# Mixture of softmaxes: the first exponential of the first two units writes the output tile, and two early loads wait for less

## The chip, the cores and the metric

One core of one Trainium2 chip. The metric is the device time of one execution in microseconds. All runs here are of the fast state, at a granted clock of 1.0. The kernel before takes 780.76 us (median of 3, 780.73 to 780.80).

## The reference

```python
batch, seq, vocab, num_heads = 32, 128, 4096, 4
# logits (32, 128, 4, 4096) fp32, prior (32, 128, 4) fp32
prior_probs = softmax(prior)                       # over the 4 heads
softmax     = softmax(logits)                      # over the 4096 entries
mixture     = sum(prior_probs[..., None] * softmax, axis=2)   # (32, 128, 4096)
```

268.4 MB of logits come in and 67.1 MB go out. The reference subtracts the row maximum before the exponential; the kernel does without that on the logits.

## The kernel before

The 4096 rows (batch times sequence) are cut into U = 32 units of 128 rows, one row per partition. A unit is 128 x 4 x 4096 values, 8.39 MB. The input tile `ltile` has two slots, used in turn, so the load of unit u+2 overwrites the slot of unit u. Units 0 to 29 go this way:

```python
lt  = ltile[:, u % 2]
acc = obuf[:, u % 2]                       # output tile, two slots
es  = (lt[:, 0], ebuf1, ebuf2, ebuf3)      # where the four exponentials go
# ScalarE: es[h] = exp(lt[:, h]), row sum into dsum[:, u, h]
# VectorE: rden = 1 / dsum;  GpSimd: coeff = rden * prior probability
# VectorE: acc  = es[0] * coeff[0]                      the "scaling"  -> adds[u, 0]
#          acc += es[h] * coeff[h], h = 1, 2, 3         the "adds"     -> adds[u, h]
# SP issues the store of acc once adds[u, 3] is done
```

The first exponential is written back into the input slot itself. So the slot may only be overwritten once the scaling has read it, and that is what the next load into it waits for:

```python
ld = nc.scalar.dma_start(out=ltile[:, u % 2, h:to], in_=lg[u // J, u % J, :, h:to, :])
if u >= 2:
    only(ld, adds[u - 2, 0] if h == 0 else exps[u - 2, to - 1])   # waits for these alone
else:
    only(ld)
...
late = u + 2 < U - 3           # if late, the load is created in the next unit's loop and then
if u + 2 < U and not late:     # moved ahead of that unit's first exponential in ScalarE's stream
    load(u + 2)
```

Loads are issued from ScalarE's stream, stores (nearly all) from SP's.

The softmax here doesn't subtract the row's maximum and nothing guards it: scores larger than these inputs give would overflow.

Of the kernel before, what the change touches and what calls it, by code (L numbers as in the profile page):

```python
# [47 lines left out]
def kernel(  # L48
# [10 lines left out]
    B, S, H, V = logits.shape  # L59
# [6 lines left out]
    U = G * J  # L66
# [13 lines left out]
    def only(ins, *keep):  # L80
        for k in keep:
            tc.add_manual_dep(
                ins.ins,
                k.ins.name,
                mybir.DependencyInfo(mybir.DependencyClass.Sync, mybir.DependencyReason.DATA),
                reason="all that this instruction waits for",
            )
        tc.declare_no_dep(
            ins.ins,
            group="loop",  # L90
            keep=[k.ins for k in keep] + before.get(ins.ins.engine, []),
            reason="covered by the waits that are kept",
        )
        tc.add_to_no_dep_group("loop", ins.ins)
        before[ins.ins.engine] = [ins.ins]
        return ins
# [4 lines left out]
    exps = {}  # L101
# [3 lines left out]
    def load(u):  # L105
        if u == 0 or u >= U - 3:
            cuts = (0, 2, 3, 4) if u == U - 1 else (0, 2, 4)
        else:
            cuts = (0, H)
        for h, to in zip(cuts, cuts[1:]):  # L110
            ld = nc.scalar.dma_start(  # L111
                out=ltile[:, u % 2, h:to], in_=lg[u // J, u % J, :, h:to, :]
            )


            if u >= 2:
                only(ld, adds[u - 2, 0] if h == 0 else exps[u - 2, to - 1])
            else:
                only(ld)
            for k in range(h, to):  # L120
                loads[u, k] = ld

    def store(u, acc, eng, lo=0, hi=V):
        st = eng.dma_start(out=ov[u // J, u % J, :, lo:hi], in_=acc[:, lo:hi])
        stores[u] = only(st, adds[u, H - 1])
# [10 lines left out]
    dsum = cpool.tile([P, U, H], FP32, name="dsum")  # L136
    rden = cpool.tile([P, U, H], FP32, name="rden")
    coeff = cpool.tile([P, U, H], FP32, name="coeff")



    ebuf1 = cpool.tile([P, V], FP32, name="ebuf1")
    ebuf2 = psum.tile([P, V], FP32, name="ebuf2")
    ebuf3 = cpool.tile([P, V], FP32, name="ebuf3")
    obuf = cpool.tile([P, 2, V], FP32, name="obuf")

    with tc.manual_schedule():
        load(0)
        nc.sync.dma_start(out=pr, in_=pv)
        load(1)  # L150
        nc.vector.reduce_max(pmax, pr, axis=AX.X)  # L151
        nc.vector.tensor_sub(pr, pr, pmax.unsqueeze(2).to_broadcast([2 * G, P, H]))  # L152
        nc.scalar.activation(pr, pr, AF.Exp)  # L153
        nc.vector.reduce_sum(pmax, pr, axis=AX.X)  # L154
        nc.vector.reciprocal(pmax, pmax)  # L155
        nc.vector.tensor_mul(  # L156
            pn.rearrange("k h r -> k r h"), pr, pmax.unsqueeze(2).to_broadcast([2 * G, P, H])
        )
        pq = pn.rearrange("k h (p j) -> k j h p", j=J)
        for t in range(P // 32):  # L160
            c = 1 - t // 2
            nc.vector.transpose(  # L162
                pp[32 * t : 32 * (t + 1), :, :, c : c + 2 * G],
                pq[:, :, :, 32 * (t % 2) : 32 * (t % 2 + 1)],
            )

        late = False
        for u in range(U):
            bufd = u < U - 2
            lt = ltile[:, u % 2]  # L170
            acc = obuf[:, u % 2] if bufd else lt[:, 0]
            es = (lt[:, 0], ebuf1, ebuf2, ebuf3) if bufd else [lt[:, h] for h in range(H)]
            ppu = pp[:, u % J, :, 2 * (u // J) + 1]

            def exp(h, *keep):
                ex = nc.scalar.activation(  # L176
                    es[h], lt[:, h], AF.Exp, accum_out=dsum[:, u, h : h + 1]
                )
                keep = (loads[u, h],) + keep
                if bufd and u and h in (1, 2):  # L180
                    keep += (adds[u - 1, 1 if h == 1 else H - 1],)
                exps[u, h] = only(ex, *keep)

            def weigh(h, n, *keep):
                rc = nc.vector.reciprocal(rden[:, u, h : h + n], dsum[:, u, h : h + n])  # L185
                only(rc, exps[u, h + n - 1])
                mul = nc.gpsimd.tensor_mul(  # L187
                    coeff[:, u, h : h + n], rden[:, u, h : h + n], ppu[:, h : h + n]
                )
                return only(mul, rc, *keep)  # L190

            def add(h, mul, lo=0, hi=V):
                if h == 0:
                    st = nc.vector.tensor_scalar(  # L194
                        out=acc[:, lo:hi], in0=es[h][:, lo:hi], scalar1=coeff[:, u, h : h + 1],
                        scalar2=None, op0=ALU.mult,
                    )
                    adds[u, h] = only(st, mul)
                else:
                    st = nc.vector.scalar_tensor_tensor(  # L200
                        out=acc[:, lo:hi], in0=es[h][:, lo:hi], scalar=coeff[:, u, h : h + 1],
                        in1=acc[:, lo:hi], op0=ALU.mult, op1=ALU.add,
                    )
                    adds[u, h] = only(st, mul, adds[u, h - 1])



            free = (stores[u - 2],) if bufd and u >= 2 else ()

            if u < U - 4:  # L210
                sets = ((0, H),)
            elif u == U - 2:
                sets = ((0, 2), (2, 3), (3, 4))
            else:
                sets = ((0, 2), (2, 4))
            for h in range(H):
                if h == 2 and 0 < u < U - 3:
                    store(u - 1, obuf[:, (u - 1) % 2], nc.sync)
                if h == 2 and u == U - 1:
                    store(u - 1, ltile[:, (u - 1) % 2, 0], nc.scalar)  # L220
                if h == 1 and late:
                    load(u + 1)
                    pairs.append((loads[u + 1, 0].ins, exps[u, 0].ins))
                    late = False
                exp(h, *(free if sets[0][1] == H and h == H - 1 else ()))
                g = next((g for g, to in sets if to == h + 1), None)
                if g is None:
                    continue
                mul = weigh(g, h + 1 - g, *(free if g == 0 and h < H - 1 else ()))
                for k in range(g, h + 1):  # L230
                    n = 2 if u == U - 1 and k == H - 1 else 1
                    w = V // n
                    for c in range(n):
                        add(k, mul, c * w, (c + 1) * w)
                        if n > 1:
                            store(u, acc, nc.scalar, c * w, (c + 1) * w)


            late = u + 2 < U - 3
            if u + 2 < U and not late:  # L240
                load(u + 2)

            if u == U - 2:
                for k in (u - 2, u - 1):
                    store(k, obuf[:, k % 2], nc.scalar)
# [30 lines left out]
```

## Time and profile before

| | before |
|---|---|
| time | 780.76 us |
| VectorE, ScalarE busy | 66%, 61% |
| DMA packets' share of 16 engines | 99.8% |
| rate over the span | 431 GB/s |
| load of unit 2: issued, load ahead of it landed | 32.18, 41.31 us |
| load of unit 3: issued, load ahead of it landed | 58.73, 64.51 us |

The first thing to ask of such a table is whether any engine is full. The compute engines are not; the DMA engines are. "Landed" is read in this text from where ScalarE starts on the data; a packet is a piece of a transfer, moved by one of the 16 engines.

### The profile page before, as it was taken

The page shows a single profiled execution, that of the slowest core. Times are in us where ns is not written, and L with a number is a line of the kernel's source. Part 1 is how long each engine was busy: PE and PEld are TensorE (multiplying, and loading weights), DVE is VectorE, ACT ScalarE, POOL GpSimd, SP SyncE. Part 2 cuts the span into 40 slices and gives each one's busy share as a digit, 9 for nine tenths or more (in the row PEclk, how much of TensorE's full clock was granted, in tenths as well). Part 3 has the DMA queues.
Part 4 walks back from the last instruction along what each step waited for, and adds up shares of the span by engine and source line. Part 5 has one row for each costly group of instructions (what it writes and reads, how often), then busy time and mean ns, then how long its engine had stood idle before and what let it go on. Part 6 is the DMA issues. An engine that isn't in the chain of part 4 may idle for free.

```text
span 779.1 us, 620 instructions
## 1 busy us (share of the span) xinstructions
DVE 517.7 (66%) x175; ACT 472.2 (61%) x258; POOL 7.6 (1%) x41
## 2 busy tenths in 40 slices
DVE  2447865568655686556875558755577555788986
ACT  4376555765557755577555675556755567557782
POOL 0000000000000000000000000000000000000000
DMA  9999999999999999999999999999999999999998
GB/s 407 458 417 400 475 404 431 431 465 424 404 468 401 463 417 423 452 448 414 417 468 407 458 404 468 421 413 448 416 459 417 457 405 464 410 429 431 432 428 379
DMA packets 10131, 335.64 MB, mean 431 GB/s; under 512 B 1136, under 2 KB 1136, under 8 KB 1168
## 3 DMA queue, kind: packets, MB, share of 16 engines
q10 hardware_dynamic: 6048, 276.83, 82.2%
q1 hardware_dynamic: 4080, 58.79, 17.6%
q14 instruction: 3, 0.02, 0.0%
HBM read 268.50 MB, written 67.11 MB: 431 GB/s over the span
## 4 chain that ended last, share of the span: by engine, by line
DMA 60%; DVE 28%; ACT 9%; issue 2%; POOL 0%; DVEq 0%; ACTq 0%; POOLq 0%
DMA out_dram<-obuf 47%; DVE obuf L200 23%; DMA ltile<-in_logits_dram 13%; ACT ebuf L176 8%; DVE obuf L194 4%; DVE ltile L200 1%; ACT ltile L176 1%; POOL coeff L187 0%; DVE rden L185 0%; DVEq L271 0%; ACTq L111 0%; POOLq L271 0%; ACTq L176 0%
## 5 line engine op out<-in xcount | busy, mean ns | idle before, releaser
L200 DVE SCALAR_TENSOR_TENSOR obuf<-ebuf,coeff,obuf 128x4096 f32<-128x4096 f32 x90 | 403.6, 4484 | 3.8 <-POOL coeff L187 0.6
L176 ACT ACTIVATE ebuf<-ltile 128x4096 f32<-128x4096 f32 x90 | 324.1, 3601 | 33.3 <-DVE obuf L200 19.4
L176 ACT ACTIVATE ltile<-ltile 128x4096 f32<-128x4096 f32 x38 | 137.4, 3615 | 255.4 <-DMA ltile<-in_logits_dram 255.0
L185 DVE RECIPROCAL rden<-dsum 128x4 f32<-128x4 f32 (+2 forms) x37 | 6.4, 174 | 235.9 <-ACT ebuf L176 233.2
L194 DVE TENSOR_SCALAR obuf<-ltile,coeff 128x4096 f32<-128x4096 f32 x30 | 70.6, 2353 | 10.9 <-POOL coeff L187 10.9
L200 DVE SCALAR_TENSOR_TENSOR ltile<-ltile,coeff 128x4096 f32<-128x4096 f32 (+1 forms) x7 | 27.0, 3874 | 1.0 <-POOL coeff L187 0.9
L176 ACT ACTIVATION_READ_ACCUMULATOR ebuf<-ltile 128x1 f32 x90 | 16.8, 187 | 0.0
L187 POOL TENSOR_TENSOR coeff<-rden,pp 128x4 f32<-128x4 f32 (+2 forms) x37 | 7.4, 201 | 756.2 <-DVE rden L185 745.6
L176 ACT ACTIVATION_READ_ACCUMULATOR ltile<-ltile 128x1 f32 x38 | 7.1, 186 | 0.0
L194 DVE TENSOR_SCALAR ltile<-ltile,coeff 128x4096 f32<-128x4096 f32 x2 | 4.7, 2353 | 0.6 <-POOL coeff L187 0.6
L153 ACT ACT_TABLE_LOAD x1 | 1.3, 1283 | 2.2 <-issue 2.2
L151 DVE TENSOR_REDUCE pmax<-pr 32x128 f32<-32x512 f32 x1 | 0.7, 674 | 2.5 <-DMA pr<-in_prior_dram 2.5
L162 DVE STREAM_TRANSPOSE pp<-pn 32x256 f32<-32x256 f32 x4 | 1.7, 435 | 0.1
L154 DVE TENSOR_REDUCE pmax<-pr 32x128 f32<-32x512 f32 x1 | 0.7, 674 | 0.7 <-ACT pr L153 0.7
L156 DVE TENSOR_TENSOR pn<-pr,pmax 32x512 f32<-32x512 f32 x1 | 1.0, 1019 | 0.0
L155 DVE RECIPROCAL pmax<-pmax 32x128 f32<-32x128 f32 x1 | 0.9, 941 | 0.0
L153 ACT ACTIVATE pr<-pr 32x512 f32<-32x512 f32 x1 | 0.6, 628 | 0.5 <-DVE pr L152 0.5
L152 DVE TENSOR_TENSOR pr<-pr,pmax 32x512 f32<-32x512 f32 x1 | 0.7, 679 | 0.0
L260 POOL MEMSET const-bfloat16-1.0<- 128x1 bf16 x1 | 0.1, 102 | 0.0
L260 POOL MEMSET const-uint8-127<- 128x1 uint8 x1 | 0.1, 102 | 0.0
L260 POOL MEMSET const-float32-0.0<- 128x1 f32 x1 | 0.1, 99 | 0.2 <-issue 0.2
L260 POOL MEMSET const-float32-1.0<- 128x1 f32 x1 | 0.1, 99 | 0.0
## 6 DMA issues: line engine op xcount, KB each, us to landing
out_dram<-obuf SPq DMA_DIRECT2D x28, 2048.0 KB, 28.1
ltile<-in_logits_dram ACTq DMA_DIRECT2D x7, 4096.0 KB, 25.5
ltile<-in_logits_dram ACTq DMA_DIRECT2D x2, 2048.0 KB, 30.9
out_dram<-obuf ACTq DMA_DIRECT2D x2, 2048.0 KB, 26.6
out_dram<-ltile ACTq DMA_DIRECT2D x1, 2048.0 KB, 19.3
out_dram<-ltile ACTq DMA_DIRECT2D x2, 1024.0 KB, 4.8
ltile<-in_logits_dram ACTq DMA_DIRECT2D x28, 29.6
pr<-in_prior_dram SPq DMA_DIRECT2D x1, 64.0 KB, 2.5
```

The source lines that it names most:

```text
L151: nc.vector.reduce_max(pmax, pr, axis=AX.X)
L152: nc.vector.tensor_sub(pr, pr, pmax.unsqueeze(2).to_broadcast([2 * G, P, H]))
L153: nc.scalar.activation(pr, pr, AF.Exp)
L154: nc.vector.reduce_sum(pmax, pr, axis=AX.X)
L155: nc.vector.reciprocal(pmax, pmax)
L156: nc.vector.tensor_mul(pn.rearrange("k h r -> k r h"), pr, pmax.unsqueeze(2).to_broadcast([2 * G, P, H]))
L162: nc.vector.transpose(pp[32 * t : 32 * (t + 1), :, :, c : c + 2 * G], pq[:, :, :, 32 * (t % 2) : 32 * (t % 2 + 1)],)
L176: ex = nc.scalar.activation(es[h], lt[:, h], AF.Exp, accum_out=dsum[:, u, h : h + 1])
L185: rc = nc.vector.reciprocal(rden[:, u, h : h + n], dsum[:, u, h : h + n])
L187: mul = nc.gpsimd.tensor_mul(coeff[:, u, h : h + n], rden[:, u, h : h + n], ppu[:, h : h + n])
L194: st = nc.vector.tensor_scalar(out=acc[:, lo:hi], in0=es[h][:, lo:hi], scalar1=coeff[:, u, h : h + 1], scalar2=None, op0=ALU.mult,)
L200: st = nc.vector.scalar_tensor_tensor(out=acc[:, lo:hi], in0=es[h][:, lo:hi], scalar=coeff[:, u, h : h + 1], in1=acc[:, lo:hi], op0=ALU.mu ...
```

## The change

The intent: if the first exponential of units 0 and 1 goes to the output tile, VectorE no longer has to read the input slot at all. The slot is free once ScalarE has done its four exponentials, and the loads of units 2 and 3 can be issued ahead of reciprocal, coefficient and scaling. For units 0 and 1 the output tile's slots are unused so far, so the new target needs no wait.

```diff
-            if u >= 2:
+            if u in (2, 3):
+                only(ld, exps[u - 2, H - 1])
+            elif u > 3:
                 only(ld, adds[u - 2, 0] if h == 0 else exps[u - 2, to - 1])
...
-            es = (lt[:, 0], ebuf1, ebuf2, ebuf3) if bufd else [lt[:, h] for h in range(H)]
+            if bufd:
+                es = (lt[:, 0] if u > 1 else acc, ebuf1, ebuf2, ebuf3)
+            else:
+                es = [lt[:, h] for h in range(H)]
...
-            late = u + 2 < U - 3
+            late = 2 <= u and u + 2 < U - 3
```

## The prediction

> **What bounds the kernel now.** I read the page first for shares of busy time, then the DMA queues, the chain that ended last, the timeline of the first 110 us, the stage table around the two loads that the change moves, and last the end of the timeline.
>
> From the page:
>
> ```profile
> DVE 517.7 (66%) x175; ACT 472.2 (61%) x258; POOL 7.6 (1%) x41
> ...
> DMA  9999999999999999999999999999999999999998
> ...
> q10 hardware_dynamic: 6048, 276.83, 82.2%
> q1 hardware_dynamic: 4080, 58.79, 17.6%
> ...
> HBM read 268.50 MB, written 67.11 MB: 431 GB/s over the span
> ...
> DMA 60%; DVE 28%; ACT 9%; issue 2%; POOL 0%; DVEq 0%; ACTq 0%; POOLq 0%
> ```
>
> No compute engine is over 66%, and the DMA digit is 9 in every slice but the last. The two queues' packets fill 82.2 + 17.6 = 99.8% of what 16 DMA engines have in 779.1 us, so at most 0.2%, some 1.6 us, isn't packet time. Adding up the trace's packet records in steps of 0.25 us says where that is: nothing moves in the first 1.0 us, the engines run dry after 776.75 us, and between 2 us and 774 us they are idle for 0.04 us on average. So this is a kernel bound by its bytes: 335.6 MB at 431 GB/s is 779 us. The chain's 28% on VectorE is not a second bound: the chain follows one store (2 MB, about 28 us to land because it shares the engines with an 8 MB load), then one unit's scale and adds, and so on. While VectorE is on the chain, the engines are moving the next unit's load.
>
> The timeline shows the two loads in question (columns: start, duration, engine, line and operation, idle before and what ended it):
>
> ```profile
> 29.08 0.19 ACT L176 ACTIVATION_READ_ACCUMULATOR ebuf<-ltile 128x1 f32 x1
> 29.30 0.18 DVE L185 RECIPROCAL rden<-dsum 128x4 f32<-128x4 f32 x1 [20.19 <-ACT ebuf L176]
> 29.56 0.20 POOL L187 TENSOR_TENSOR coeff<-rden,pp 128x4 f32<-128x4 f32 x1 [29.12 <-DVE rden L185]
> 29.79 2.35 DVE L194 TENSOR_SCALAR obuf<-ltile,coeff 128x4096 f32<-128x4096 f32 x1 [0.32 <-POOL coeff L187]
> 32.18 0.33 ACTq L111 DMA_DIRECT2D ltile<-in_logits_dram  x1
> ...
> 41.31 3.62 ACT L176 ACTIVATE ltile<-ltile 128x4096 f32<-128x4096 f32 x1 [12.04 <-DMA ltile<-in_logits_dram]
> ...
> 55.63 0.18 ACT L176 ACTIVATION_READ_ACCUMULATOR ebuf<-ltile 128x1 f32 x1
> ...
> 58.73 0.33 ACTq L111 DMA_DIRECT2D ltile<-in_logits_dram  x1
> ...
> 64.51 3.62 ACT L176 ACTIVATE ltile<-ltile 128x4096 f32<-128x4096 f32 x1 [8.70 <-DMA ltile<-in_logits_dram]
> ```
>
> The load of unit 2 is issued at 32.18, once unit 0's scaling has read the first quarter of the input slot. But the load of unit 1 (8 MB, queued since the first microseconds) only lands at 41.31, where ScalarE starts on unit 1. So unit 2's load has stood 41.3 - 32.2 = 9.1 us in the queue behind unit 1's before its own bytes can move. The load of unit 3 is issued at 58.73, and unit 2's lands at 64.51: again 5.8 us of overlap. The engines do not run out of load packets in either place. The stage table (length, busy times, clock, DMA share, GB/s):
>
> ```profile
> 32.20:41.30 9.10, 9.03 (x3) 0.00 (x0) 0.00 (x0) 1.00 1.06 461
> ...
> 59.00:65.00 6.00, 5.96 (x2) 0.49 (x1) 0.00 (x0) 1.00 1.17 481
> ```
>
> The short stages swing between 0.76 and 1.17 because a packet is booked whole in the stage in which it starts; two neighbours average out to about 1.
>
> **What the Trainium skill says.** (1) "DMA: Bandwidth & Descriptors", section "Where 436 GB/s comes from": 16 ports of 32 B at 850 MHz give 435.2 GB/s. This trace: 431 GB/s over the whole span, 99% of it, start and end included; it agrees, and leaves under 1%. (2) The same page, "Queues, rings and completion order": each engine takes packets in turn from the queue rows that have work, and within one ring descriptors are consumed in order. The trace agrees in so far as an 8 MB load and a 2 MB store overlap throughout. So a load put in earlier behind another load of the same ring should start no sooner. (3) "Perfetto Trace Analysis", section "DMA Instruction — HWDGE (DVE, Sync)": the issue's record covers descriptor generation, not the movement. The trace: 0.33 us per issue, about 29.6 us until a full load lands; the moment of issue isn't the moment of transfer. (4) "VectorE: DVE Perf Modes", "The perf-mode tier table": an fp32 tensor_scalar in SBUF is in the 2x tier, a two-tensor operation at 1x. The trace: 2353 ns and 4484 ns for 128x4096.
>
> **The change part by part.**
>
> - *Target of the first exponential.* In units 0 and 1 it writes the output tile, not the input slot in place. The count and order of instructions on every engine stay as they were (I compared the two builds: the same 173 VectorE rows, the same ScalarE sequence, other operands). ScalarE: 2 instructions of 3.6 us either way: the page has 3601 ns for writes to another buffer and 3615 ns in place. No new wait: nothing has used the output tile before unit 0 or 1. Cost 0.
> - *Scaling in place.* VectorE now reads and writes the output tile. Both operands stay fp32 in SBUF; the page has 2353 ns for obuf<-ltile and 2353 ns for ltile<-ltile. Cost 2 x 0 = 0.
> - *Wait of loads 2 and 3.* They wait for the fourth exponential instead of the scaling. Removed from the path to the issue: reciprocal, coefficient product, scaling and the small gaps between. Load 2: from the end of the accumulator read at 29.08 + 0.19 = 29.27 to 32.18, so 2.9 us earlier; load 3: from 55.81 to 58.73, 2.9 us earlier. Both are beside a transfer of the same queue that still has 9.1 and 5.8 us to go; that time in the queue becomes 12.0 and 8.7 us. On the path: 0.
> - *ScalarE freed earlier.* The issue stands in ScalarE's own stream and blocks it while it waits. But the next exponential needs the load that lands at 41.31 (or 64.51), so ScalarE's 12.04 and 8.70 us of waiting merely end on another instruction. Gain 0.
> - *The two loads leave the delayed placement* (`late`). That placement already put them ahead of the next unit's first exponential; the built order shows the same position. Cost 0.
>
> Sum: 0 us by these steps, and at most the 0.04 us of engine idle in the middle. The 1.0 us ahead of the first packet and the 2.4 us after the engines run dry are not touched.
>
> **The rivals.**
>
> - *A hidden gap before loads 2 and 3 is closed.* Were the engines idle from landing to issue, both loads would gain up to 2.9 us each: 5.8 us, to 775.0. Against it: the loads are issued before their predecessors land, and the sum of packets shows full engines from 32 to 65 us. I give it 2%.
> - *Deeper load queue crowds out the stores.* With two loads queued instead of one, store 0 (from 45.74 us) might get a smaller share, unit 2's reuse of buffers might wait, and time is lost. Against it: one nonempty load queue or a longer one is the same to a turn-taking engine, and any bytes that a store loses, a load gains. Even a store of 2 MB a few us later costs nothing while bytes bound the time. It would leave 780.8, give or take 0.5.
> - *A shift in the pattern reaches the end.* The second-last store is issued at 771.02, while the engines are still on the store issued at 754.06 (19.3 us to landing: 773.4), so VectorE has about 2.3 us of margin there. A pattern shifted by more than that would open a gap, up to 1 or 2 us: 782. For it: stores and loads interleave closely, so a shift can propagate. Against it: issues only get earlier, and nothing slows VectorE.
> - *VectorE or ScalarE become the bound.* With 66% and 61% busy and no added work, no.
>
> **Range and chances.** The predicted time is 780.7 us, the median before, 780.76, less the 0.04 us. The three runs before differ by 0.07 us, the profiled execution was 780.91. I widen that to 780.1 to 781.4 for a different interleaving of packets and for the end effect. Two per cent is 15.6 us, more than four times what the DMA engines leave unused in all at both ends (3.4 us); faster by that much would need fewer bytes or a higher rate, slower by that much would need some 16 us of idle engines. So 0.005 each, and 0.99 for the same.
>
> **What would show it right or wrong.** In the changed profile, the two issues should stand at about 29.3 and 55.8 us, unit 1's first exponential still at 41.3 and unit 2's at 64.5 (each to 0.3 us), store 0's issue at 45.7, the queues' shares together still 99.8%, the scaling of units 0 and 1 at 2.35 us. If unit 2's exponential comes more than 1 us earlier, the hidden gap was real and I am wrong; if the loads land as before but the stores' time to landing rises, the crowding rival holds. What would break the prediction: packets that take longer than the 2.42 us per 64 KB seen in this trace, or an engine that ran dry late in the kernel.

## The result

780.85 us (median of 6, 780.72 to 781.00) beside 780.75 (median of 6) for the kernel before: ratio 1.0002, 95% interval 0.9989 to 1.0015, the same. Here and below the ratio is the mean time of one kernel's fast runs over that of the other's of the same rounds, so it is not quite the ratio of the medians quoted.

The page of the changed kernel: engines, DMA slices, queues, and the two new operations.

```profile
DVE 517.6 (66%) x175; ACT 472.2 (61%) x258; POOL 7.6 (1%) x41
...
DMA  9999999999999999999999999999999999999998
...
q10 hardware_dynamic: 6048, 276.83, 82.3%
q1 hardware_dynamic: 4080, 58.79, 17.6%
...
L182 ACT ACTIVATE obuf<-ltile 128x4096 f32<-128x4096 f32 x2 | 7.2, 3616 | 19.9 <-DMA ltile<-in_logits_dram 19.9
...
L200 DVE TENSOR_SCALAR obuf<-obuf,coeff 128x4096 f32<-128x4096 f32 x2 | 4.7, 2354 | 0.6 <-POOL coeff L193 0.6
```

The change is there (two exponentials into the output tile, two scalings in place on it) and costs nothing: 3616 and 2354 ns each. The shares are those of before.

Its timeline around the two loads:

```profile
29.24 0.33 ACTq L111 DMA_DIRECT2D ltile<-in_logits_dram  x1
...
41.25 3.62 ACT L182 ACTIVATE obuf<-ltile 128x4096 f32<-128x4096 f32 x1 [12.04 <-DMA ltile<-in_logits_dram]
...
55.79 0.33 ACTq L111 DMA_DIRECT2D ltile<-in_logits_dram  x1
...
64.60 3.62 ACT L182 ACTIVATE ltile<-ltile 128x4096 f32<-128x4096 f32 x1 [8.84 <-DMA ltile<-in_logits_dram]
```

Both issues come 2.9 us earlier, as intended: 29.24 for 32.18 and 55.79 for 58.73. What depends on the data does not: ScalarE begins unit 1 at 41.25 (41.31 before) and unit 2 at 64.60 (64.51 before). The packet records say the same more closely. A full load is 128 packets of 64 KB; counted in order of time, the 129th such packet, where unit 2's load takes over from unit 1's, starts at 40.36 us before and 40.44 after, and the 257th at 64.37 and 64.35. The loads wait longer in the queue, and that is all.

### The profile page after: what moved, and what is told of

Read it like the earlier page. It is cut to its first block, busy times and chain, and to the rows that moved or that the text cites. A ratio compares the mean times of both kernels' runs of the same rounds, so it can differ in the third digit from the quotient of the medians.

```text
span 779.0 us, 620 instructions
## 1 busy us (share of the span) xinstructions
DVE 517.6 (66%) x175; ACT 472.2 (61%) x258; POOL 7.6 (1%) x41
## 4 chain that ended last, share of the span: by engine, by line
DMA 60%; DVE 28%; ACT 9%; issue 2%; POOL 0%; DVEq 0%; ACTq 0%; POOLq 0%
DMA out_dram<-obuf 47%; DVE obuf L206 23%; DMA ltile<-in_logits_dram 13%; ACT ebuf L182 8%; DVE obuf L200 4%; DVE ltile L206 1%; ACT obuf L182 0%; POOL coeff L193 0%; DVE rden L191 0%; DVEq L277 0%; ACT ltile L182 0%; ACTq L111 0%; POOLq L277 0%; ACTq L182 0%
## 5 line engine op out<-in xcount | busy, mean ns | idle before, releaser
L182 ACT ACTIVATE ltile<-ltile 128x4096 f32<-128x4096 f32 x36 | 130.1, 3614 | 235.7 <-DMA ltile<-in_logits_dram 235.3
L200 DVE TENSOR_SCALAR obuf<-ltile,coeff 128x4096 f32<-128x4096 f32 x28 | 65.9, 2353 | 10.3 <-POOL coeff L193 10.3
L182 ACT ACTIVATE obuf<-ltile 128x4096 f32<-128x4096 f32 x2 | 7.2, 3616 | 19.9 <-DMA ltile<-in_logits_dram 19.9
L200 DVE TENSOR_SCALAR obuf<-obuf,coeff 128x4096 f32<-128x4096 f32 x2 | 4.7, 2354 | 0.6 <-POOL coeff L193 0.6
```

Source lines behind the costliest of these rows:

```text
L182: ex = nc.scalar.activation(es[h], lt[:, h], AF.Exp, accum_out=dsum[:, u, h : h + 1])
L200: st = nc.vector.tensor_scalar(out=acc[:, lo:hi], in0=es[h][:, lo:hi], scalar1=coeff[:, u, h : h + 1], scalar2=None, op0=ALU.mult,)
```

## The experiments

Theory ("bytes"): the DMA engines are full from the first microsecond to the last few, so only an event that empties them, or changes the bytes, moves the time. An issue counts only if it comes too late to follow the load ahead of it. Rivals: the earlier issue gains and the new target loses as much; the moment of issue counts by itself; the chain of store, exponentials and adds sets the pace; ScalarE's stream, which the issue blocks, is what matters.

Two sums over the packet records are used below. *Idle* is time in which engines had no packet, averaged over the 16. *Long packets* is what packets took above their usual time (2.418 us for 64 KB, 1.2135 for 32 KB, 0.611 for 16 KB; for 48 KB, which one experiment has, 1.8155 put in between), divided by 16. In the kernel before, idle is under 0.02 us between 2 and 774 us, and long packets come to 1.4 us. The trace kept here does not name a packet's engine, so idle is counted from the number of packets in flight (16 less that number, where it is under 16). Packet records overlap a little, up to 19 at once in the kernel before. Each trace is of one execution, and its time is not always near the median: where that matters, the text says so.

| run | median us | ratio to before (95%) |
|---|---|---|
| target_only | 780.86 | 1.0000 (0.9988 to 1.0013) |
| after_again | 780.88 | 1.0001 (0.9988 to 1.0013) |
| fewer_adds | 780.89 | 1.0001 (0.9987 to 1.0015) |
| load2_last_add | 787.43 | 1.0086 (1.0072 to 1.0099) |
| load3_last_add | 789.89 | 1.0116 (1.0102 to 1.0130) |
| exp1_late | 781.50 | 1.0015 (1.0001 to 1.0029) |
| second_add | 782.31 | 1.0018 (1.0005 to 1.0031) |
| load2_second_add | 780.74 | 1.0000 (0.9987 to 1.0012) |
| load3_second_add | 782.16 | 1.0011 (0.9998 to 1.0025) |
| load2_three_heads | 778.20 | 0.9966 (0.9954 to 0.9979) |
| three_heads_again | 778.25 | 0.9969 (0.9956 to 0.9981) |
| after_three_heads | 778.69 | 0.9972 (0.9959 to 0.9984) |

Five runs each, four for load2_last_add and load3_last_add.

### One half alone, and the change again

```diff
 # target_only: kernel before
-            es = (lt[:, 0], ebuf1, ebuf2, ebuf3) if bufd else ...
+            es = (lt[:, 0] if u > 1 else acc, ebuf1, ebuf2, ebuf3) if bufd else ...
```

> The kernel before with one half of the change: the first exponential of units 0 and 1 writes the output tile, the loads of units 2 and 3 still wait for the scaling. Bytes theory: 780.75 us, ratio 1.000 within 0.001; load 2 issued at 32.2, load 3 at 58.7, scaling in place 2.35 us. Rival (the earlier loads gain and the new target loses the same): slower than before by up to 5.8 us, ratio up to 1.007.

> The changed kernel once more, beside runs of the kernel before on the same chip. Bytes theory: ratio 1.000 within 0.001. A real loss of the size of the first measurement would show as 1.0002 again, which is below what these runs tell apart.

Both came out as before. So the new target loses nothing that an earlier load could have won back, and the first rival falls. The other half, the earlier load without the new target, would overwrite what the scaling still has to read; it was not run alone (its result would be wrong, though a time could be had). The step from target_only to after_again is that half on top of the first: 780.86 and 780.88.

### Is the chain the bound?

```diff
 # fewer_adds: kernel before, the second head's add left out in units 0 to 29 (wrong result on purpose)
                 for k in range(g, h + 1):
                     ...
+                    if k == 1 and bufd:
+                        adds[u, k] = adds[u, 0]
+                        continue
```

> The kernel before without the second head's add in units 0 to 29 (wrong result on purpose): 30 VectorE operations of 4.48 us fewer, 134.5 us of its 518. Bytes theory: 780.75, ratio 1.000 within 0.002. Rival (the chain that ended last is the bound: it passes through the adds of every second unit): 15 x 4.5 us, 67 us faster, about 713, ratio 0.91.

VectorE's busy time fell by 134.5 us and the time by nothing. The page's engine line, and the chain that ended last (share of the span by line), of this experiment:

```profile
DVE 383.2 (49%) x145; ACT 466.4 (60%) x258; POOL 7.6 (1%) x41
```

```profile
by line: DMA ltile<-in_logits_dram 64.4%; ACT ebuf L176 19.6%; ACT ltile L176 7.4%; DVE obuf L194 4.2%; issue 1.5%; DVE ltile L200 0.9%; POOL coeff L187 0.4%; DVE rden L185 0.4%; DVEq L274 0.3%; ACTq L111 0.1%; POOLq L274 0.0%; ACTq L176 0.
```

Before, 47% of the chain was stores and 28% VectorE. Now 64.4% is loads, the adds of units 0 to 29 (`obuf`, line 200) have left it altogether, and the span is 778.9 us for 779.1. A chain names one path of several that are equally long; where the same engines serve all the paths, their shares do not say what shortening one of them is worth.

### What a really late load costs

```diff
 # load2_last_add: kernel before (load3_last_add: the same with u == 3 and adds[1, H - 1])
-            if u >= 2:
+            if u == 2:
+                only(ld, adds[0, H - 1])
+            elif u > 2:
                 only(ld, adds[u - 2, 0] if h == 0 else exps[u - 2, to - 1])
```

> The kernel before, load 2 alone waits for unit 0's last add: issue at 45.7 us, 4.4 us after load 1 has landed at 41.3, store 0 comes no earlier than 45.7 either. Bytes theory: the DMA engines run dry from 41.3 to about 46.7 (issue plus some 1 us to the first packet), and since bytes bound the rest the loss is never recovered: 5.4 us slower, 786.1 (785 to 787), ratio 1.007. Rival (the loop of store, exponentials and adds sets the pace, or later slack takes it up): 780.75 to 782.

> The kernel before, load 3 alone waits for unit 1's last add: issue at 72.3 us, 7.8 us after load 2 has landed at 64.5. Unlike in load2_last_add a store is in flight then: store 0 has some 0.4 MB left, which fills about 1 us. Bytes theory: engines dry from about 65.5 to 73.3, 7.8 us slower, 788.5 (787 to 790), ratio 1.010. Rival (what was lost is taken up later): under 1.003.

The stage table of the kernel before (length, busy times of VectorE, ScalarE and GpSimd, clock, DMA share, GB/s), then that of load2_last_add, then that of load3_last_add:

```profile
38.00:42.00 4.00, 3.96 (x2) 0.69 (x1) 0.00 (x0) 1.00 1.17 508
42.00:46.00 4.00, 3.71 (x1) 4.00 (x3) 0.00 (x0) 1.00 1.21 524
...
62.00:66.00 4.00, 3.96 (x2) 1.49 (x1) 0.00 (x0) 1.00 0.91 393
66.00:72.00 6.00, 5.96 (x2) 5.83 (x4) 0.00 (x0) 1.00 1.01 437
```

```profile
38.00:42.00 4.00, 3.96 (x2) 0.00 (x0) 0.00 (x0) 1.00 0.57 246
42.00:46.00 4.00, 3.65 (x1) 0.00 (x0) 0.00 (x0) 1.00 0.00 0
```

```profile
62.00:66.00 4.00, 3.96 (x2) 0.00 (x0) 0.00 (x0) 1.00 0.62 262
66.00:72.00 6.00, 5.96 (x2) 0.00 (x0) 0.00 (x0) 1.00 0.00 0
```

Here the DMA share does fall to 0.00, and it costs. In load2_last_add the idle sum between 38 and 48 us is 5.94 us, and the long packets come to 0.6 us more than before: together 6.5, and the median is 6.6 slower (787.43 less 780.80). The traced execution is the slowest of the four, 787.90, 7.0 above the traced one of the kernel before (780.91); 0.3 us more idle at the end (from 774 us on) belongs to it. In load3_last_add the idle sum is 7.6 us, long packets 1.6 more: 9.2, measured 9.1. Nothing is taken up later. Both missed my expectation by 1.2 to 1.3 us. Of load2_last_add's miss, half is the gap (from the last packet's end at 40.9, and for some engines earlier, to the first new one at 46.5, not from 41.3), half the long packets; of load3_last_add's, all is long packets.

### Is it the load or ScalarE that is late?

In load2_last_add the blocked issue also holds up ScalarE. So the same delay was put on ScalarE alone:

```diff
 # exp1_late: changed kernel
+                if u == 1 and h == 0:
+                    keep += (adds[0, H - 1],)
                 exps[u, h] = only(ex, *keep)
```

> The changed kernel, with unit 1's first exponential made to wait for unit 0's last add, at 45.7 us in place of 41.3; load 2 is issued at 29.3 as before. It takes from load2_last_add the late ScalarE and leaves out the late load. Bytes theory: load 3 is issued at about 60.2, before load 2 lands at 64.5, so 780.8, ratio 1.000 within 0.001. Rival (load2_last_add is slow because ScalarE's stream is held up): 4.4 us slower, ratio 1.0056.

781.50 (five runs, 781.42 to 783.32): 0.7 us slower, not 4.4, and not the 0.0 that I expected either. The engines are not idle (0.01 us between 2 and 774 us, as good as before); the profiled execution has 0.6 us more of long packets, in the stretches at 105, 130, 155 and 180 us. So it is the late load that costs nearly all of the time in load2_last_add. That the packets grow longer when ScalarE's part of the pattern shifts is seen here; why is not settled.

### How close may an issue come?

```diff
 # second_add: kernel before (load2_second_add: u == 2 alone; load3_second_add: u == 3 alone)
-            if u >= 2:
+            if u in (2, 3):
+                only(ld, adds[u - 2, 1])
+            elif u > 3:
                 only(ld, adds[u - 2, 0] if h == 0 else exps[u - 2, to - 1])
```

> The kernel before with loads 2 and 3 moved the other way, each waiting one VectorE operation more (the first add after the scaling): issues at 36.7 and 63.2 us in place of 32.2 and 58.7. Bytes theory: still ahead of the landings at 41.3 and 64.5, so 780.75, ratio 1.000 within 0.001, engines full. Rival (the moment of issue counts, each us of it): 9 us slower, ratio 1.0115.

> Half of second_add: load 2 alone waits for the second VectorE operation, issue at 36.6, 4.7 us ahead of load 1's landing at 41.3. Theory A (only an issue too close to the landing of the load ahead of it disturbs): 780.8, as before. Theory B (any later issue costs): at least half of second_add's 1.5 us, 781.5 or more.

> The other half: load 3 alone, issue at 63.1, 1.4 us ahead of load 2's landing at 64.5. Theory A: all of second_add's loss is here, 781.2 to 782.8, without idle engines, with a further set of 16 long packets after 65 us. Theory B: about half of it, 781.5. A third way, that second_add's loss was chance: 780.8.

second_add came out 1.5 us slower, where the bytes theory had 0 and the rival 9. Its halves show which load costs it. Load 2 issued at 36.65, still 4.6 us ahead of the landing: 780.74, nothing. Load 3 issued at 63.1, 1.4 us ahead of it: 782.16, 1.4 us slower. (The interval of load3_second_add, 0.9998 to 1.0025, just takes in 1; but all five runs, 781.10 to 782.61, lie above every run of before in that series, 780.90 at most.)

The timelines of load2_second_add and then of load3_second_add:

```profile
36.65 0.33 ACTq L111 DMA_DIRECT2D ltile<-in_logits_dram  x1
...
41.26 3.62 ACT L178 ACTIVATE ltile<-ltile 128x4096 f32<-128x4096 f32 x1 [12.04 <-DMA ltile<-in_logits_dram]
```

```profile
63.12 0.33 ACTq L111 DMA_DIRECT2D ltile<-in_logits_dram  x1
...
64.54 3.62 ACT L178 ACTIVATE ltile<-ltile 128x4096 f32<-128x4096 f32 x1 [8.85 <-DMA ltile<-in_logits_dram]
```

So a later issue as such costs nothing. That nearness to the landing is what counts fits both halves, but they also differ in which load is late. The packet records show what nearness did: in load3_second_add unit 2's last packet ends at 63.50, 0.4 us after the issue, and unit 3's first full packet starts at 65.42, where it was 64.37 before; in load2_second_add unit 2's first starts at 40.38 (40.36 before). Load 3 was 1.05 us late, yet the engines didn't run dry then: store 0's packets filled the time (idle 0.00 us from 60 to 68 us).

What the time went to shows in part: in second_add a full set of 16 long packets, of 2.7 to 3.0 us in place of 2.42, near 84 us, where the kernel before has none (its two sets come near 48 and 60 us). But that trace is of second_add's fastest run, 781.17, with long packets 0.5 us above those of before; of the other four, at 782.2 to 782.8, there is no trace. The runs of these two kernels also scatter more, second_add from 781.17 to 782.76. In the profiled execution of load3_second_add, 782.61, its slowest and 1.7 above that of the kernel before, long packets come to 0.85 us more than before, and a hole opens near the end as well, 0.6 us of idle between 772 and 774 us. Why the packets grow longer is open.

### A kernel in which the change has something to do

```diff
 # load2_three_heads, three_heads_again: kernel before; after_three_heads: changed kernel
 # (wrong result on purpose: unit 2's fourth head keeps what was in the slot)
-            cuts = (0, H)
+            cuts = (0, H if u != 2 else H - 1)
...
-            for k in range(h, to):
+            for k in range(h, H if u == 2 else to):
                 loads[u, k] = ld
```

> The kernel before, unit 2's load brings three heads of four, so 2.10 MB fewer of 335.64 (wrong result on purpose). Bytes theory: 2.10 MB at 432 GB/s is 4.85 us: 775.9, ratio 0.9938. Rival (chain of stores and VectorE sets the pace): 780.75, ratio 1.000.

2.10 MB fewer bring 2.6 us, not 4.85. The chain rival, which had 0, falls; but I had overlooked that a load that is shorter by 4.85 us also uses up the 5.8 us of slack ahead of load 3. The timeline of load2_three_heads shows it:

```profile
58.66 0.34 ACTq L111 DMA_DIRECT2D ltile<-in_logits_dram  x1
...
59.04 3.62 ACT L176 ACTIVATE ltile<-ltile 128x4096 f32<-128x4096 f32 x1 [3.29 <-DMA ltile<-in_logits_dram]
```

Load 3 is issued 0.4 us before ScalarE has unit 2's data, and by the packet records 0.8 us after the last of unit 2's packets (57.90); its own first packet starts at 60.45. The store in flight fills most of that time. The idle sum from 59 to 64 us is 0.5 us, long packets are 1.4 us more than before, and 0.2 us of idle stands near the end: 4.85 - 0.5 - 1.4 - 0.2 is some 2.7, which is what the two profiled executions differ by (780.91 and 778.24). This is the situation that the change was made for.

> The kernel before with three heads of unit 2 loaded, repeated as the base of after_three_heads. The first time it took 778.20 us, 2.6 less than before and not the 4.85 of its bytes: load 2 landed at 59.0, load 3 was issued at 58.66, the engines were idle for 0.5 us on average from 60.5 to 62, and some 64 KB packets took 2.6 to 3.9 us in place of 2.42. Expected: 778.2 within 0.2, the same idle time.

> The changed kernel with three heads of unit 2 loaded (wrong result on purpose). Here the slack that hides the change is used up: load 2 lands at about 59.0, load 3 is issued at 55.8 and not at 58.7. Bytes theory: the idle of 0.5 us from 60.5 to 62 is gone, so about 0.6 us faster than three_heads_again, some 777.6, more if the long packets go with it (up to 776). Rival (the moment of issue has no effect at all, or the new target costs something): 778.2 or more, the idle still there.

The timeline of after_three_heads, and the last stretches of three_heads_again and then of after_three_heads (stage table, columns as above):

```profile
55.85 0.33 ACTq L111 DMA_DIRECT2D ltile<-in_logits_dram  x1
...
59.15 3.62 ACT L182 ACTIVATE ltile<-ltile 128x4096 f32<-128x4096 f32 x1 [3.33 <-DMA ltile<-in_logits_dram]
```

```profile
764.00:768.00 4.00, 3.96 (x2) 0.00 (x0) 0.00 (x0) 1.00 1.00 430
768.00:770.00 2.00, 2.00 (x2) 0.00 (x0) 0.00 (x0) 1.00 0.69 291
```

```profile
764.00:768.00 4.00, 3.96 (x2) 0.00 (x0) 0.00 (x0) 1.00 0.97 418
768.00:770.00 2.00, 2.00 (x2) 0.00 (x0) 0.00 (x0) 1.00 0.33 139
```

Load 3 is issued 3.3 us ahead of the landing, and the idle time from 59 to 64 us is gone (0.31 us in three_heads_again, 0.00 here). The change does what it says. Yet the median is 778.69, not below 778.25; the five runs spread from 777.59 to 779.27, so one came out as expected and four did not. With such a spread the 0.4 us between the two medians are not clear of noise. The profiled execution, 779.27 and the slowest of the five, shows where it went there: the hole from 768 to 770.5 us, where the engines have done all that was queued and VectorE has not yet finished the last unit, has grown from 0.48 to 1.33 us of idle, and long packets by 0.2. Together 0.85 + 0.2 - 0.3 = 0.75 us slower, measured 0.95 between the two profiled executions. That accounts for one execution; for the others there is no trace.

No kernel here is faster than the one before with a correct result. What is left to win at this rate is small: of the 779.1 us span the idle sum takes 3.2 us, 1.2 at the start and 2.0 at the end; for the rest all 16 engines have packets of bytes that have to be moved.

## Why the prediction was right

780.85 lies in the range of 780.1 to 781.4, 0.15 above the point, a difference that says nothing: the 0.04 us of gain in the sum (under 0.02 by the count used here) can't be seen in runs that differ by 0.2 to 0.3. By its own steps:

- *The bound.* Right, and now shown from both sides: less VectorE work brings nothing (fewer_adds), fewer bytes bring time (load2_three_heads), engines run dry cost their idle time in full (load2_last_add, load3_last_add). One reading was wrong on the way: 99.8% for the queues does not mean that at most 1.6 us is free of packets. Packet records overlap, by 2.4 us when summed over 16 engines, so the sum hides part of the 3.2 us that are free at the two ends. The prediction's own 1.0 and 2.4 us at the ends say the same; nothing in the forecast hung on it.
- *The two issues 2.9 us earlier, the landings unmoved.* Forecast 29.3, 55.8, 41.3 and 64.5; measured 29.24, 55.79, 41.25 and 64.60.
- *New target and scaling in place, cost 0.* 3616 and 2354 ns; target_only has ratio 1.0000.
- *Slack of 9.1 and 5.8 us.* Load 2 took 4.5 us of its slack for nothing in load2_second_add. Load 3's did not hold to its end: 1.4 us ahead of the landing already costs about 1.4 us at the median. The slack was counted to ScalarE's start, which is 0.4 and 1.0 us too long against the last packet of the load ahead, and an issue needs time until its first packet: in load2_last_add, with idle engines, 0.87 us for the store (45.67 to 46.54) and 1.8 us for the load issued beside it (45.68 to 47.46).
- *Rivals.* The hidden gap, an idle stretch that the earlier issue would close, is excluded by the packet records of both kernels. Crowded-out stores are excluded too: median 28.1 us to landing in both kernels. The shifted end did not occur in the changed kernel (last issues at 770.90 for 771.02), but it is real: it is what took the gain in the profiled run of after_three_heads, and I had given it a fair size, 1 to 2 us.
- *What I left out.* I took the bytes' rate as fixed. It is so in the steady part, where the 64 KB packets take 2.418 us on average; in the first 300 us, long packets come and go with the interleaving, up to 1.7 us more in sum than in the kernel before. In this change they stayed alike (1.38 and 1.45 us), so the forecast was spared. That part was luck: nothing in the prediction showed that they would.

## What to carry to other kernels

Before moving an issue earlier, find the landing of the transfer ahead of it in the same queue. Here an issue 4.6 us or more before it gained nothing by coming sooner; load 3, issued 1.4 us before it, lost about 1.4 us at the median, and loads issued after it lost 6.6 and 9.1 us. Where the line runs between 1.4 and 4.6 us was not tried. When the DMA engines are full throughout, look at bytes and idle engines first, then at packets that take longer (up to 1.7 us here); add up the packets before believing a chain of waits. And a gap closed early may be lost again at the end of the kernel, as in the one traced run of after_three_heads.

## What the Trainium skill lacked or had wrong

- "DMA: Bandwidth & Descriptors", "Rules for kernel authors", advises to issue a DMA early to overlap it. It has no word on when earlier stops helping: here 9.1 and 5.8 us ahead of the preceding load's landing were as good as 12.0 and 8.8, 4.6 us was as good for load 2, and 1.4 us cost about 1.4 us for load 3.
- The same page, "Latency and other measured facts", has some 600 ns to the first byte for a hardware-generated DMA. Here, with idle engines, 0.87 us passed from the start of a store's issue (45.67) to its first packet (46.54), and 1.8 us for the load issued beside it (45.68 to 47.46).
- The same page, "Where 436 GB/s comes from", says that for transfers between HBM and SBUF the HBM side's 358 GB/s binds, though the same section calls its own measurement of 425 near fabric rate. This lone core held 431 GB/s over the whole span, loads and stores together, 1% below the 435.2 of the fabric. The skill has this right elsewhere: "HBM Reference", "Specifications (TRN2)", says that a core which streams alone measures well above its share of 358.
- No page speaks of packets that take longer for a while: in the kernel before two sets of 16, near 48 and 60 us, of 2.7 to 3.0 us for 64 KB in place of 2.418; after a disturbed interleaving more of them, of up to 3.9 us (load2_three_heads) and as late as 290 us (after_three_heads). The cause is open.
